# Key scales widened later, and another order of projections and mixer rows, in a hybrid decoder block

## The chip, the cores and the metric

The program runs on one core of one Trainium2 chip. The metric is the time of one execution in microseconds (us). A time is the median of several executions; beside it stand the lowest and the highest. A profile is one further execution, recorded by the hardware profiler, with a time of its own.

The engines of the core are named as the profile names them: PE (TensorE, matmuls and transposes; PEld its weight loads), DVE (VectorE), ACT (ScalarE), POOL (GpSimd) and SP (which issues nearly all DMAs).

## What is computed

One layer of a decoder on 512 tokens of width 2048, all float32. `h = rms_norm(x)` is multiplied by one matrix of 30 column tiles of 128; their outputs feed three token mixers:

```python
proj = h @ w_in[l]
aq, ak, av, bu, bg, cq, ck, cv = jnp.split(proj, splits, axis=-1)
aq = _rms_norm(aq.reshape(B, S, A_HEADS, HEAD_DIM), a_q_g[l])
ak = _rms_norm(ak.reshape(B, S, A_HEADS, HEAD_DIM), a_k_g[l])
out_a = _dilated_mixture(aq, ak, av)              # 8 heads of 64, three dilations
out_b = _conformer_conv(bu, bg, ...)              # GLU, 31 taps, layer norm, silu
cq, ck = (_rms_norm(...) for both)
out_c = _band_attention(cq, ck, cv, 127, sinks)   # 16 query heads, 2 key heads
mix = jnp.concatenate([out_a, out_b, out_c], axis=-1)
x = x + mix @ w_out[l]
h2 = _rms_norm(x, norm2_g[l])
x = x + (silu(h2 @ w_gate[l]) * (h2 @ w_up[l])) @ w_down[l]
```

Queries and keys are normalised per head: each is divided by the root of the mean of its own squares. This is the "scale" in what follows.

## The kernel before

Activations lie transposed: 128 channels on the partitions, 512 tokens along a row. A float32 product is made of three matmuls on a high and a low part of each operand (`mm3`, lines 312 to 314: high weights by high data, high by low, low by high). ACT makes a high part by rounding, and DVE (POOL for the C rows of the mixer) makes the low part by subtracting it.

**Projections.** `PROJ` is the order of the 30 column tiles: a letter for the mixer, a letter for the kind (q, k, v, u, g) and a number. The first four run ahead. Each of the others is a loop over 16 k tiles, three matmuls each (`project`). The host lays out the weights in the order of `PROJ`, so the loads stay a straight stream in whatever order it stands.

**Ticks.** Everything that is not a projection is hung between its matmuls by a clock written out by hand. After every second k tile (six matmuls) `project` calls `ticks.tick()`, and `ticks.after(n, fn)` makes `fn` issue its instructions n ticks from now. A projection has 8 ticks. Each engine runs its instructions in the order in which they were issued, and waits where an operand isn't there.

**A key tile** (`do_k`, with `head_scales`) is a chain of such steps: ACT copies the tile out of PSUM (L564, `raw`); SQ = 3 ticks later PE transposes it (L569, `f`); then one tick each: ACT squares (L574), DVE sums per head (L579, L581), POOL raises the sums to the power -1/2 (L586, `r`). Then `then(r)` hangs up the widening: ACT spreads each scale over the 64 channels of its head (L623, `wide`); a tick later PE transposes that (L630, `t`), a tick later DVE multiplies the raw keys by it (L636), a tick later SP copies each half to the other partitions (L642, the twin, two DMAs), and TD = 2 ticks later ACT and DVE make the high and the low part (L648, L653). `box["k at"]` tells the heads the tick from which they may use the key. A query tile (`do_q`) is split without its scale (L602, L607, four DMAs L609, L610), which goes into the exponent instead.

**Heads.** C heads come in pairs of query tiles that share a key (`grouped_attention`), A heads one tile at a time (`attention`): scores on PE (L755 to L758), maxima on DVE (L770 to L786), exps on ACT (L796), denominators on DVE (L803 to L808), normalising on POOL (L811, L814), transposes on PE (L846, L916), their high and low parts (L852, L857; L921, L927, L933), and the product with the values (L870, L871, L946). A head starts at the earliest tick at which its key, its query and its values are ready and the head before it is far enough ahead. Names: `a1o` is the output of A tile 1, `a1pl` the low part of its weights, `a10s` the scores of its head 0, `ml_c` the low part of a mixer row tile of C. PSUM has six rotating banks for all this, and a seventh and eighth for the projections; an allocation waits for the last reader of the bank that it gets.

**Output projection.** `ROWS` is the order in which the 16 row tiles of the mixed output enter the contraction with `w_out` (again the host lays the weights out in this order). The first eight form half 0, the others half 1. The first two output tiles run together (`first_two`), one tick after each k, which is six matmuls; after them four k tiles, 12 matmuls, go to a tick. `split_rows(k)` makes the high and low parts of rows k to k + 2 that exist by then. Rows ahead of that are split during the last projection.

Past the mixer come the feed-forward matmuls (lines 1255 and 1397), to which the change does nothing.

Of the kernel before, what the change touches and what calls it, by code (L numbers as in the profile page):

```python
# [36 lines left out]
PAUSE_FROM, TAP_PAUSE = 205, 9  # L37


SQ, VD, TD, EV = 3, 4, 2, 1  # L40


C_TICKS = (1, 6, 2, 2, 2, 2, 4, 1, 5)
# [1 line left out]


PROJ = ("av0 av1 av2 av3 bu0 bg0 cv ck cq0 cq3 bu1 bg1 cq1 cq5 cq2 "
        "cq7 bu2 bg2 ak2 cq4 cq6 bu3 bg3 ak0 aq0 ak1 aq1 aq2 ak3 aq3").split()
ROWS = "c0 c1 c2 c4 c5 c3 c7 c6 a0 a1 b2 b1 b0 b3 a2 a3".split()

N_SLOTS = 67
N_WIDE = 4
# [70 lines left out]
def kernel(ctx: ExitStack, tc: tile.TileContext, xT, wi, wo, wgu, wd, cst_in, outT):  # L123
# [19 lines left out]
    ticks = Ticks()  # L143

    def slot(name, dt=F32, cols=T):
        return sp.tile([P, cols], dt, name=name, tag="s")
# [4 lines left out]
    def bank(name, cols=T):  # L151
        return psum["banks"].tile([P, cols], F32, name=name, tag="b")
# [116 lines left out]
    at = {"entry": 0, "split": 0, "use": 0}  # L269
# [208 lines left out]
    def project(name):  # L478
        b = column(name)
        for half in range(2):  # L480
            wh, wl = next_unit()
            for kk in range(8):
                k = 8 * half + kk
                s = slice(kk * P, (kk + 1) * P)
                mm3(b, wh[:, s], wl[:, s], h_hi[k], h_lo[k], k == 0, k == KT - 1)
                if kk % 2 == 1:
                    ticks.tick()
        return b
# [61 lines left out]
    def ln_out(mix):  # L550
# [3 lines left out]
        for j in range(NB):  # L554
            nc.scalar.activation(yconv[j], yconv[j], AF.Silu, bias=col(C_LB + j), scale=col(C_LG + j))
            mix[f"b{j}"] = yconv[j]
        for n, name in enumerate(r for r in ROWS if r[0] == "b"):
            ticks.after(1 + n, split_mix, name)


    def head_scales(b, name, then):

        raw = slot(name + "raw")
        nc.scalar.copy(raw, b)  # L564

        def flip():
            b2 = bank(name + "f")
            for i in range(NT):
                nc.tensor.transpose(b2[:, i * P:(i + 1) * P], raw[:, i * P:(i + 1) * P], ident)  # L569
            ticks.after(1, square, b2)  # L570

        def square(b2):
            sq = slot(name + "sq")
            nc.scalar.activation(sq, b2, AF.Square)  # L574
            ticks.after(1, total, sq)

        def total(sq):
            v = cp.tile([P, NT, 2], F32, name=name + "v", tag="hsv", bufs=3)
            nc.vector.tensor_reduce(v.rearrange("p a b -> p (a b)"), sq.rearrange("p (a b) -> p a b", b=HD),  # L579
                                    axis=mybir.AxisListType.X, op=ALU.add)  # L580
            nc.vector.tensor_add(v, v, c64[:, :, None].to_broadcast([P, NT, 2]))  # L581
            ticks.after(1, power, v)

        def power(v):
            r = cp.tile([P, NT, 2], F32, name=name + "r", tag="hsr", bufs=4)
            nc.gpsimd.tensor_tensor(r, v, nhalf.rearrange("p (a b) -> p a b", b=2), op=ALU.pow)  # L586
            then(r)

        ticks.after(SQ, flip)
        return raw  # L590

    def do_q(box, b, name):
        def then(r):
            box["rq"] = r

        raw = head_scales(b, name, then)
        box["q at"] = ticks.now + SQ + 4
        q = box["q"] = [slot(f"{name}{h}", F32R) for h in range(2)]

        def high():  # L600
            hi = slot(f"{name}hi", F32R)
            nc.scalar.copy(hi, raw)  # L602
            ticks.after(1, low, hi)

        def low(hi):
            lo = slot(f"{name}lo", F32R)
            nc.vector.tensor_sub(lo, raw, hi.bitcast(F32))  # L607
            for h in range(2):
                nc.sync.dma_start(q[h][HALF[h]].bitcast(F32), hi[HALF[h]].bitcast(F32))  # L609
                nc.sync.dma_start(q[h][HALF[1 - h]].bitcast(F32), lo[HALF[h]].bitcast(F32))  # L610
        ticks.after(1, high)

    def do_k(box, b, name, gi):
        def then(r):
            ticks.after(2, widen, r)

        raw = head_scales(b, name, then)
        box["k at"] = ticks.now + SQ + TD + 10
        both = []

        def widen(r):
            wide = slot(name + "wide")
            nc.scalar.copy(wide.rearrange("p (a b c) -> p a b c", a=NT, b=2),  # L623
                           r[:, :, :, None].to_broadcast([P, NT, 2, HD]))
            ticks.after(1, flip, wide)

        def flip(wide):
            b2 = bank(name + "t")
            for i in range(NT):
                nc.tensor.transpose(b2[:, i * P:(i + 1) * P], wide[:, i * P:(i + 1) * P], ident)  # L630
            ticks.after(1, scale, b2)

        def scale(b2):
            for h in range(2):
                both.append(slot(f"{name}{h}"))
                nc.vector.scalar_tensor_tensor(both[h][HALF[h]], raw[HALF[h]], gqk[HALF[h], gi:gi + 1], b2[HALF[h]],  # L636
                                               op0=ALU.mult, op1=ALU.mult)
            ticks.after(1, twin)

        def twin():  # L640
            for h in range(2):
                nc.sync.dma_start(both[h][HALF[1 - h]], both[h][HALF[h]])  # L642
            ticks.after(TD, high)

        def high():
            box["k"] = [(slot(f"{name}h{h}", F32R), slot(f"{name}l{h}", F32R)) for h in range(2)]
            for h in range(2):
                nc.scalar.copy(box["k"][h][0], both[h])  # L648
            ticks.after(1, low)

        def low():
            for h, (hi, lo) in enumerate(box["k"]):
                nc.vector.tensor_sub(lo, both[h], hi.bitcast(F32))  # L653
            if gi == 1:
                box["k0"] = [slot(f"{name}0{h}", F32R, 2 * P) for h in range(2)]
                for k0, src in zip(box["k0"], both):
                    nc.scalar.copy(k0[:, :P], src[:, :P])
                    nc.vector.tensor_sub(k0[:, P:], src[:, :P], k0[:, :P].bitcast(F32))
# [327 lines left out]
    def split_mix(name):  # L986
        if name not in m_hi:
            m = mix.pop(name)
            hi, lo = slot(f"mh_{name}", F32R), slot(f"ml_{name}", F32R)
            nc.scalar.copy(hi, m)  # L990
            (nc.gpsimd if name[0] == "c" else nc.vector).tensor_sub(lo, m, hi.bitcast(F32))  # L991
            m_hi[name], m_lo[name] = hi, lo
# [26 lines left out]
    for name in PROJ[HEAD4:]:  # L1019
        kind, what, j = name[0], name[1], name[2:]  # L1020
        if name == PROJ[-1]:
            for n, row in enumerate(ROWS[:2]):
                ticks.after(4 + n, split_mix, row)
        b = project(name)
        if kind == "b":
            ticks.after(0, glu if what == "g" else glu_u, int(j), b)
            continue
        if kind == "c":
            box = Heads(shared) if j else shared
        else:  # L1030
            box = boxes.setdefault(j, {})
        if what == "k":
            do_k(box, b, name, 1 if kind == "c" else 0)
        elif what == "v":
            do_v(box, b, name)
        else:
            do_q(box, b, name)
        if what == "q":
            if kind == "a":
                load_v(box, int(j))  # L1040
                attention(boxes.pop(j), kind + j)
                continue
            waiting.append((box, kind + j, (int(j), int(j) + 8)))
            if len(waiting) == 2:
                grouped_attention(waiting)
                waiting = []
# [6 lines left out]
    def load_x(i):  # L1053
        if i < KT:
            n = OUT_ORDER[0][i]
            xr[n] = slot(f"xr{n}")
            nc.sync.dma_start(xr[n], xT[n])
# [79 lines left out]
    def split_rows(k):  # L1137
        for name in ROWS[k:k + 3]:
            if name in mix:
                split_mix(name)  # L1140

    def first_two(*ns):
        two = [((bank if i else column)(f"o0_{n}"), *next_unit(SPLIT_AHEAD - i)) for i, n in enumerate(ns)]
        for k in range(8):
            row = ROWS[k]
            while row not in m_hi and row not in mix:
# [13 lines left out]
    for half in range(2):  # L1160
        for i, n in enumerate(OUT_ORDER[half]):
# [12 lines left out]
            for kk in range(8):  # L1174
                if half == 1 and i == KT - 2 and kk == 4:
                    first_sum[0][0]()
                k = 8 * half + kk
                row = ROWS[k]
                while row not in m_hi and row not in mix:
# [7 lines left out]
            if half == 0:  # L1187
                load_x(i + 2)
                if i >= 8 and ROWS[i] in mix:
                    split_mix(ROWS[i])  # L1190
# [337 lines left out]
    for g in range(2 * NP + N_DOWN):  # L1528
# [8 lines left out]
        for i, q in enumerate(ORDER):  # L1537
# [35 lines left out]
            if N_TURNED - 2 <= t < N_TURNED:  # L1573
                n = 4 - (t % 2 == 0)
# [91 lines left out]
```

## Time and profile before

| | |
|---|---|
| median of 3 runs | 1879.83 us (1879.47 to 1881.76) |
| profiled execution | 1881.01 us, of which the recorded span is 1879.0 |
| granted clock, mean | 0.998 |
| projections and mixer | to about 400 us |
| output projection | about 399 to 610 us |

The span is the time from the first to the last recorded instruction; the execution has 2.0 us around it. The views used below are: the page's busy times and chain; the waits of PE (which instruction stood idle, and which engine's instruction released it); the timelines, in which a row has the start and the duration in us, the engine, the line, the operation, out<-in, and in brackets the idle time before it and its releaser; windows, which give for a stretch of time the busy us and the count of instructions of PE, PEld, DVE, ACT and POOL, the clock granted to PE as a share of full speed (PEclk), the busy share of the DMA engines and GB/s; and groups of equal instructions (busy us in all, mean ns of one, idle before).

### The profile page before, as it was taken

What the parts mean: (1) busy time and instruction counts of PE and PEld (TensorE: products, weight loads), DVE (VectorE), ACT (ScalarE), POOL (GpSimd) and SP (SyncE); (2) the same over time, 40 slices, a digit from 0 to 9 for tenths busy, and PEclk for the clock granted to TensorE, in tenths of its full rate; (3) what the DMA queues carried; (4) which work ended last, traced back from release to release, by engine and by line L of the source; (5) the groups of instructions that cost most, each with busy time, mean ns of one, the idle gap of its engine ahead of it and who ended that gap; (6) DMA issues with size and microseconds to landing.
All of it is one profiled execution on the core that took longest, in us unless ns stands there. A gap on an engine that the chain in (4) does not pass through costs nothing.

```text
span 1879.0 us, 28424 instructions
## 1 busy us (share of the span) xinstructions
PE 1868.2 (99%) x9784; PEld 1605.4 (85%) x9784; DVE 1458.2 (78%) x2347; ACT 1333.2 (71%) x1886; POOL 1219.5 (65%) x812
## 2 busy tenths in 40 slices
PE   9999999999999999999999999999999999999999
PEld 7888878888888888888888888888888888888888
DVE  7578988997679777777777777777777677778887
ACT  6345545553556888888878888788887887777675
POOL 5014433462155878787877878788787867766786
PEclk9999999999999999999999999999999999999999
DMA  7333332434342354443544435344455475578984
GB/s 271 122 110 108 93 96 85 126 100 145 107 146 88 120 175 145 157 168 130 182 138 163 163 133 183 134 164 161 142 178 192 152 239 184 197 251 285 308 243 124
DMA packets 157984, 301.07 MB, mean 160 GB/s; under 512 B 29968, under 2 KB 69008, under 8 KB 157840
## 3 DMA queue, kind: packets, MB, share of 16 engines
q1 hardware_dynamic: 157696, 299.25, 48.4%
q8 instruction: 77, 1.26, 0.3%
q14 instruction: 67, 0.55, 0.1%
q10 hardware_dynamic: 144, 0.01, 0.0%
HBM read 241.27 MB, written 50.33 MB: 155 GB/s over the span
## 4 chain that ended last, share of the span: by engine, by line
PE 92%; DVE 5%; ACT 1%; issue 1%; POOL 1%; DMA 0%; DVEq 0%; POOLq 0%; ACTq 0%
PE out L1255 51%; PE out L1397 16%; PE o L313 3%; PE o L314 3%; PE o L312 3%; DVE wl L290 1%; PE cq L312 1%; PE cq L314 1%; PE cq L313 1%; DVE y L514 1%; PE in L313 1%; PE in L312 1%; PE in L314 1%; PE ak L314 1%; PE ak L312 1%
## 5 line engine op out<-in xcount | busy, mean ns | idle before, releaser
L1255 PE MATMUL out<-h,wh 128*128 128x512 f32 x2464 | 588.4, 391 | 0.0
L1255 PEld LDWEIGHTS out<-h,wh 128*128 128x128 f32 x2464 | 452.7, 188 | 87.5
L1255 PEld LDWEIGHTS out<-h,wl 128*128 128x128 f32 x2464 | 316.1, 191 | 12.5 <-DVE wl L295 0.4
L1255 PE MATMUL out<-h,wl 128*128 128x256 f32 x2464 | 320.3, 283 | 0.2 <-DVE wl L295 0.2
L1397 PE MATMUL out<-wh,a 128*128 128x512 f32 x896 | 221.2, 389 | 0.0
L1397 PEld LDWEIGHTS out<-wh,a 128*128 128x128 f32 x896 | 168.2, 188 | 34.9
L289 ACT CAST wh<-w 128x1024 fp32r<-128x1024 f32 (+1 forms) x93 | 96.8, 1042 | 129.3 <-PE o L313 43.2
L290 DVE TENSOR_TENSOR wl<-w,wh 128x1024 fp32r<-128x1024 f32 (+1 forms) x93 | 117.1, 1261 | 44.9 <-ACT wh L289 44.5
L1397 PE MATMUL out<-wl,a 128*128 128x512 f32 x448 | 119.7, 389 | 0.0
L1397 PEld LDWEIGHTS out<-wl,a 128*128 128x128 f32 x448 | 84.1, 188 | 17.4
L514 DVE SCALAR_TENSOR_TENSOR y<-bu,cst,y 128x511 f32<-128x511 f32 (+14 forms) x120 | 94.4, 787 | 0.7
L1255 PE MATMUL out<-a,wh 128*128 128x512 f32 x330 | 80.1, 391 | 0.0
L1255 PEld LDWEIGHTS out<-a,wh 128*128 128x128 f32 x330 | 60.3, 188 | 11.4
L312 PE MATMUL o<-mh_c,wh 128*128 128x512 f32 x128 | 51.2, 400 | 0.0
L313 PE MATMUL o<-ml_c,wh 128*128 128x512 f32 x128 | 50.1, 392 | 0.5 <-POOL ml_c L991 0.5
L314 PE MATMUL o<-mh_c,wl 128*128 128x512 f32 x128 | 50.1, 391 | 0.0
L1442 DVE TENSOR_TENSOR Y<-Y,out 128x512 f32<-128x512 f32 x48 | 30.7, 682 | 19.4 <-PE out L1397 19.3
L1255 PEld LDWEIGHTS out<-a,wl 128*128 128x128 f32 x330 | 43.3, 191 | 2.2
L1255 PE MATMUL out<-a,wl 128*128 128x256 f32 x330 | 44.1, 283 | 0.0
L312 PE MATMUL cq<-hh,wh 128*128 128x512 f32 x96 | 39.3, 410 | 0.0
L430 POOL TENSOR_TENSOR ssum<-ssum,sq 128x512 f32<-128x512 f32 x15 | 26.8, 1785 | 19.1 <-ACT sq L429 18.6
L314 PE MATMUL cq<-hh,wl 128*128 128x512 f32 x96 | 38.3, 399 | 0.0
(3395 smaller groups left out, 5170.7 us busy)
## 6 DMA issues: line engine op xcount, KB each, us to landing
od<-a SPq DMA_DIRECT2D x140, 256.0 KB, 4.7
a<-od SPq DMA_DIRECT2D x140, 256.0 KB, 6.4
w<-in_wi SPq DMA_DIRECT2D x59, 512.0 KB, 3.6
w<-in_wo SPq DMA_DIRECT2D x32, 512.0 KB, 3.5
x<-in_xT SPq DMA_DIRECT2D x16, 256.0 KB, 7.4
xr<-in_xT SPq DMA_DIRECT2D x16, 256.0 KB, 3.7
x2d<-xr SPq DMA_DIRECT2D x16, 256.0 KB, 2.0
yd<-z SPq DMA_DIRECT2D x16, 256.0 KB, 5.3
```

Of the source, the lines that this page charges most:

```text
L289: nc.scalar.copy(hi[:, :n], t[:, :n])
L290: eng.tensor_sub(lo[:, :n], t[:, :n], hi[:, :n].bitcast(F32))
L312: nc.tensor.matmul(out, wh, xh, start=start, stop=False)
L313: nc.tensor.matmul(out, wh, xl, start=False, stop=False)
L314: nc.tensor.matmul(out, wl, xh, start=False, stop=stop)
L430: eng.tensor_add(acc, acc, sq)
L514: nc.vector.scalar_tensor_tensor(yconv[j][:, i:], hconv[j][:, :T - i], c, yconv[j][:, i:], op0=ALU.mult, op1=ALU.add)
L1255: nc.tensor.matmul(out, lhs[:, s], rhs, start=begin, stop=last and low == flip[0] and x is xs[-1], skip_group_check=True)
L1397: nc.tensor.matmul(to[h], x[:, h * P:(h + 1) * P], v[:, j], start=sub == 0 and h not in started, stop=sub == 1 and n in (len(todo) - 1, le ...
L1442: nc.vector.tensor_add(t, t, b)
```

## The change

The widening of every key's scales is hung up KW = 5 ticks after the power instead of 2, and `box["k at"]` counts these ticks, so it stands 20 ticks after the projection instead of 15. In `PROJ` ak0 goes ahead of bu3 and bg3, aq2 ahead of ak3, and aq1 behind ak3. In `ROWS` the C rows stand in the order of the pairs of query tiles (c0 c3, c1 c5, c2 c7, c4 c6), and of the A rows a2 goes ahead of a1. During the last projection three rows are split, at ticks 1, 3 and 5, instead of two, at ticks 4 and 5. No operation is added or removed.

```diff
-SQ, VD, TD, EV = 3, 4, 2, 1
+SQ, KW, VD, TD, EV = 3, 5, 4, 2, 1
...
 PROJ = ("av0 av1 av2 av3 bu0 bg0 cv ck cq0 cq3 bu1 bg1 cq1 cq5 cq2 "
-        "cq7 bu2 bg2 ak2 cq4 cq6 bu3 bg3 ak0 aq0 ak1 aq1 aq2 ak3 aq3").split()
-ROWS = "c0 c1 c2 c4 c5 c3 c7 c6 a0 a1 b2 b1 b0 b3 a2 a3".split()
+        "cq7 bu2 bg2 ak2 cq4 cq6 ak0 bu3 bg3 aq0 ak1 aq2 ak3 aq1 aq3").split()
+ROWS = "c0 c3 c1 c5 c2 c7 c4 c6 a0 a2 b2 b1 b0 b3 a1 a3".split()
...
     def do_k(box, b, name, gi):
         def then(r):
-            ticks.after(2, widen, r)
+            ticks.after(KW, widen, r)
 
         raw = head_scales(b, name, then)
-        box["k at"] = ticks.now + SQ + TD + 10
+        box["k at"] = ticks.now + SQ + KW + TD + 10
...
         if name == PROJ[-1]:
-            for n, row in enumerate(ROWS[:2]):
-                ticks.after(4 + n, split_mix, row)
+            for n, row in enumerate(ROWS[:3]):
+                ticks.after(1 + 2 * n, split_mix, row)
```

What it does to the order is shown at two places. The first is ACT's queue at ak2's widening (`ak2wide`), in the middle of the C heads; `c71` is the second head of C tile 7 and `cq4` a query tile. Before:

```order
L564 COPY cq4raw_2511<-cq4_2357 128x512
L289 CAST wh43_2516<-w43_1973 128x1024
L623 COPY ak2wide_2528<-ak2r_2494 128x512
L796 ACTIVATE c71e0_2503,c71d_1899<-c71s1_2467,c71d_1899,cq7r_2037 128x128 x2
L798 ACTIVATE c71d_1899<-c71d_1899,cst_75 128x2
L602 CAST cq4hi_2543<-cq4raw_2511 128x512
L289 CAST wh44_2599<-w44_2059 128x1024
```

After the change:

```order
L564 COPY cq4raw_2511<-cq4_2357 128x512
L289 CAST wh43_2516<-w43_1973 128x1024
L796 ACTIVATE c71e0_2503,c71d_1899<-c71s1_2467,c71d_1899,cq7r_2037 128x128 x2
L798 ACTIVATE c71d_1899<-c71d_1899,cst_75 128x2
L602 CAST cq4hi_2541<-cq4raw_2511 128x512
L623 COPY ak2wide_2581<-ak2r_2494 128x512
L289 CAST wh44_2588<-w44_2059 128x1024
```

ak2wide stands behind the exps of c71 and the rounding of cq4 instead of ahead of them. PE's queue at the transposes of it (`ak2t`), before:

```order
L313 MATMUL cq6_2515<-h3_188,wh41_2358 128x512
L314 MATMUL cq6_2515<-h3_188,wl41_2359 128x512
L630 MATMUL ak2t_2545<-ident_110,ak2wide_2528 128x128 x4
L312 MATMUL cq6_2515<-hh4_214,wh41_2358 128x512
L313 MATMUL cq6_2515<-hl4_215,wh41_2358 128x512
L314 MATMUL cq6_2515<-hh4_214,wl41_2359 128x512
```

and after the change:

```order
L946 MATMUL c20o1_2569<-c20bh1_2474,cvd0_855 128x256 x2
L946 MATMUL c20o1_2569<-c20bl1_2492,cvd0_855 128x256 x2
L569 MATMUL cq4f_2583<-ident_110,cq4raw_2511 128x128 x4
L312 MATMUL cq6_2515<-hh8_311,wh42_2426 128x512
L313 MATMUL cq6_2515<-hl8_312,wh42_2426 128x512
L314 MATMUL cq6_2515<-hh8_311,wl42_2427 128x512
L312 MATMUL cq6_2515<-hh9_338,wh42_2426 128x512
L313 MATMUL cq6_2515<-hl9_339,wh42_2426 128x512
L314 MATMUL cq6_2515<-hh9_338,wl42_2427 128x512
L630 MATMUL ak2t_2605<-ident_110,ak2wide_2581 128x128 x4
L312 MATMUL cq6_2515<-hh10_359,wh42_2426 128x512
L313 MATMUL cq6_2515<-hl10_360,wh42_2426 128x512
```

ak2t has moved behind the rest of that half of cq6's projection, behind the products of head 0 of the C pair c2, c7 (`c20o`), the transposes of cq4 and six more matmuls.

The second place is DVE's queue early in the output projection, where the second A head pair's weights get their low parts. Before, this pair is a1's and the scores beside it are a2's:

```order
L781 ISA a20s2_4092,a20d_3688<-a20s2_4092,bias_a_122 128x512
L781 ISA a20d_3688 128x1
L784 SCALAR_TENSOR_TENSOR a20d_3688<-a20d_3688,aq2r_3841 128x1
L607 TENSOR_TENSOR aq3lo_4130<-aq3raw_4019,aq3hi_4095 128x512
L636 SCALAR_TENSOR_TENSOR ak30_4136<-ak3raw_3855,gqk_124,ak3t_4097 64x512
L636 SCALAR_TENSOR_TENSOR ak31_4138<-ak3raw_3855,gqk_124,ak3t_4097 64x512
L675 TENSOR_TENSOR av30_4124<-av3s_4023,av30_4124 128x4x64
L675 TENSOR_TENSOR av31_4125<-av3s_4023,av31_4125 128x4x64
L884 TENSOR_TENSOR mix_a1_4128<-mix_a1_4128,a1o0_4080 64x512
L806 SCALAR_TENSOR_TENSOR a20e1_4155,a20d_3688<-a20e1_4155,mult_a_121 128x384
L808 RECIPROCAL a20d_3688<-a20d_3688 128x1
L857 TENSOR_TENSOR a1pl10_4194<-a1t10_4112,a1ph10_4162 128x512
```

After the change the pair is a2's and the scores are a1's:

```order
L607 TENSOR_TENSOR aq3lo_4144<-aq3raw_4033,aq3hi_4111 128x512
L884 TENSOR_TENSOR mix_a2_4113<-mix_a2_4113,a2o0_4076 64x512
L806 SCALAR_TENSOR_TENSOR a10e0_4132,a10d_3856<-a10e0_4132,mult_a_121 128x128
L806 SCALAR_TENSOR_TENSOR a10e0_4132,a10d_3856<-a10e0_4132,mult_a_121 128x256
L808 RECIPROCAL a10d_3856<-a10d_3856 128x2
L781 ISA a10s2_4135,a10d_3856<-a10s2_4135,bias_a_122 128x512
L781 ISA a10d_3856 128x1
L784 SCALAR_TENSOR_TENSOR a10d_3856<-a10d_3856,aq1r_4022 128x1
L675 TENSOR_TENSOR av30_4138<-av3s_4037,av30_4138 128x4x64
L675 TENSOR_TENSOR av31_4139<-av3s_4037,av31_4139 128x4x64
L857 TENSOR_TENSOR a2pl10_4180<-a2t10_4104,a2ph10_4142 128x512
L857 TENSOR_TENSOR a2pl11_4198<-a2t11_4127,a2ph11_4176 128x512
```

The scaling of ak3 (L636) is no longer here, and the first low part of the second head (`a2pl10`, before `a1pl10`) follows the two low parts of av3 at once. On PE the scores a10s2 and the transposes `aq3f`, which take the bank that a2pl10 reads, stand as follows after the change:

```order
L757 MATMUL a10s2_4135<-ak1h0_3704,aq10_3852 128x512
L758 MATMUL a10s2_4135<-ak1l0_3705,aq10_3852 128x512
L312 MATMUL o0_0_4062<-mh_c5_4094,wh61_3859 128x512
L313 MATMUL o0_0_4062<-ml_c5_4095,wh61_3859 128x512
L314 MATMUL o0_0_4062<-mh_c5_4094,wl61_3860 128x512
L312 MATMUL o0_1_4069<-mh_c5_4094,wh62_3951 128x512
L313 MATMUL o0_1_4069<-ml_c5_4095,wh62_3951 128x512
L314 MATMUL o0_1_4069<-mh_c5_4094,wl62_3952 128x512
L846 MATMUL a2t12_4161<-ident_110,a21e1_3934 128x128
L846 MATMUL a2t12_4161<-ident_110,a21e2_3987 128x128
L569 MATMUL aq3f_4171<-ident_110,aq3raw_4033 128x128 x4
L312 MATMUL o0_0_4062<-mh_c2_4117,wh61_3859 128x512
```

Before, `aq3f` took the bank of the scores a20s1, which ACT's exps read last.

## The prediction

> **What bounds the kernel now.** I read the page first (busy times, chain), then the waits of PE, then the timelines at each wait.
>
> ```profile
> PE 1868.2 (99%) x9784; PEld 1605.4 (85%) x9784; DVE 1458.2 (78%) x2347; ACT 1333.2 (71%) x1886; POOL 1219.5 (65%) x812
> ...
> PE 92%; DVE 5%; ACT 1%; issue 1%; POOL 1%; DMA 0%; DVEq 0%; POOLq 0%; ACTq 0%
> ```
>
> PE is busy for 1868.2 us of the span and carries 92% of the chain that ended last. The change leaves PE's matmuls as they are, so it can only win or lose time in which PE stands still, or runs at a lower clock. The view of PE's waits lists nearly all of the first kind (engine, line waited for: us in total, times, longest):
>
> ```profile
> core 0 of [0], span 1879.0 us
> ...
> PE ak2t L630 <- ACT ak2wide L623: 3.8, 1, 3.8
> PE idle L410 <- DVE bones L343: 1.4, 1, 1.4
> PE ak1t L630 <- ACT ak1wide L623: 0.8, 1, 0.8
> PE a10s L758 <- DVE ak1l L653: 0.8, 1, 0.8
> PE o L313 <- POOL ml_c L991: 0.5, 2, 0.3
> ```
>
> The 1.4 us are at the start, before anything that is changed. The other four lie in the mixer and at the start of the output projection, and each waits for a step that the change moves: 3.8 + 0.8 + 0.8 + 0.5 = 5.9 us. The first costs more than it shows. PE's timeline (start, duration):
>
> ```profile
> 253.75 0.39 PE L313 MATMUL cq<-h,wh 128*128 128x512 f32 x1
> 253.98 0.39 PE L314 MATMUL cq<-h,wl 128*128 128x512 f32 x1
> 258.21 1.12 PE L630 MATMUL ak2t<-ident,ak2wide 128*128 128x128 f32 x4 [3.84 <-ACT ak2wide L623]
> ...
> 263.88 0.40 PE L946 MATMUL c20o<-c20ph,cv 128*128 128x256 f32 x2
> ...
> 265.55 0.60 PE L569 MATMUL cq4f<-ident,cq4raw 128*128 128x128 f32 x4
> ...
> 391.14 0.60 PE L846 MATMUL a1t<-ident,a10e 128*128 128x128 f32 x4
> 391.57 0.60 PE L569 MATMUL ak3f<-ident,ak3raw 128*128 128x128 f32 x4
> ```
>
> A 128x512 matmul issues every 0.23 us (253.75 to 253.98; 0.2265 over longer stretches), four transposes take 0.43 us (391.14 to 391.57). Between the matmul at 253.98 and c20o stand four transposes and 12 matmuls: 0.43 + 12 x 0.2265 = 3.15 us. Without a stall c20o would start at 253.98 + 0.23 + 3.15 = 257.36; it started at 263.88, 6.5 us late. The rest beyond the 3.84 us is the clock (windows: us, busy times and counts, PEclk, DMA share, GB/s):
>
> ```profile
> 254.37:258.20 3.83, 0.00 (x0) 0.00 (x0) 3.69 (x9) 0.66 (x2) 3.13 (x2) 0.79 0.00 0
> 258.20:260.00 1.80, 1.79 (x7) 1.60 (x8) 0.27 (x2) 1.54 (x6) 0.61 (x1) 0.50 0.81 232
> ...
> 256.50:257.00 0.50, 0.00 (x0) 0.00 (x0) 0.50 (x1) 0.00 (x0) 0.50 (x1) 0.59 0.00 0
> ...
> 263.40:263.80 0.40, 0.40 (x3) 0.35 (x2) 0.00 (x0) 0.00 (x0) 0.30 (x1) 0.98 0.83 190
> ```
>
> The granted clock fell to half at about 256.6, 2.2 us after PE's last matmul ended (254.37), and came back at about 263.4. The 5.2 us of work from 258.21 on ran at half speed, which is 2.6 us lost. The wait at the start (1.4 us) and those of 0.8 us show no such drop.
>
> **The change, part by part.**
>
> *ak2's widening, three ticks later.* Why it was late:
>
> ```profile
> 254.21 1.69 POOL L933 TENSOR_TENSOR c20bl<-c20pl,mask_c 128x512 fp32r<-128x512 f32 x1 [1.36 <-DVE c20pl L927]
> 255.87 1.63 POOL L586 TENSOR_TENSOR ak2r<-ak2v,nhalf 128x8 f32<-128x8 f32 x1
> ...
> 257.54 0.62 ACT L623 COPY ak2wide<-ak2r 128x512 f32<-128x512 f32 x1 [3.49 <-POOL ak2r L586]
> 258.06 0.45 ACT L796 ACTIVATE c71e<-c71s,c71d,cq7r 128x128 f32<-128x128 f32 x1
> ...
> 259.13 0.61 ACT L602 CAST cq4hi<-cq4raw 128x512 fp32r<-128x512 f32 x1
> ```
>
> ACT stood 3.49 us on ak2r, and the exps of c71 and cq4hi were queued behind it. In the changed order both go ahead of ak2wide. They then end before ak2r does, or little after: c71e to cq4hi took 259.74 - 258.06 = 1.7 us here, from about 256.2 (when DVE ends c71's maximum) that gives 257.9. ak2wide then ends near 258.5. PE reaches ak2t only after 12 matmuls (2.72), c20o (265.55 - 263.88 = 1.67), four transposes (0.43) and 6 matmuls (1.36): 254.21 + 6.18 = 260.4. That is 1.9 us to spare; without it the wait returns by as much as ak2wide is later. Gain: 6.5 us.
>
> Where the stall goes: DVE worked for 3.69 of the 3.83 us in which PE stood, and now does that work beside PE. The next thing due is c20bl for c20o's second tile: POOL ended it at 255.90, PE wants it at about 254.2 + 2.72 + 1.4 = 258.3, 2.4 us to spare. I take nothing for it, with 2 us as the bad end.
>
> *ck three ticks later* moves the first C heads by 18 matmuls, 4.1 us. On SP's queue ck's two twin DMAs are now issued behind three weight loads instead of ahead of them, and the heads start ten ticks after, as before. The heads' mixer rows are read some 200 us later, so I take nothing; if DVE, on which their maxima wait, falls back by it, at most those 4.1 us less what the heads' spacing holds. *ak0 before bu3, bg3* brings its two scalings and two low parts (2.8 us of DVE) ahead of c40o:
>
> ```profile
> 312.77 2.87 POOL L933 TENSOR_TENSOR c40bl<-c40pl,mask_c 128x256 fp32r<-128x256 f32 x2 [1.02 <-DVE c40pl L927]
> ...
> 318.49 0.40 PE L946 MATMUL c40o<-c40bl,cvd 128*128 128x256 f32 x2
> ```
>
> POOL was done at 315.64, 2.85 us early, as much as the added work: 0 to 1 us, I take 0.2. ak0's two twin DMAs on SP go with it; aq0 is their next reader, far behind.
>
> *ak1 later, aq2 sooner, aq1 later.* ak1's transposes come 5 ticks after the power instead of 2, against a wait of 0.8; the second pair of A heads now uses ak2, whose low part is 100 us old, in place of ak1's, another 0.8. Both go: 1.6 us. aq2's DMAs are issued with aq2, as aq1's were; same distance.
>
> *Three rows split at ticks 1, 3, 5* takes one more ml_c out of POOL's full stretch behind tick 5 and puts the first two some 5 us further ahead of their matmuls: 0.5 us, or nothing if POOL falls behind again.
>
> *What the order costs.* ak3 (scaling, sums, low part) moves some 14 us up, into the stretch where DVE is fullest (two windows, then groups of DVE between 340 and 420):
>
> ```profile
> 340.00:370.00 30.00, 28.44 (x140) 23.36 (x139) 27.99 (x73) 16.29 (x30) 11.37 (x9) 1.00 0.41 115
> 370.00:395.00 25.00, 25.00 (x133) 21.20 (x132) 24.26 (x64) 12.86 (x22) 12.01 (x9) 1.00 0.30 85
> ...
> L806 DVE SCALAR_TENSOR_TENSOR a20e<-a20e,mult_a 128x128 f32<-128x128 f32 (+3 forms) x4 | 1.9, 482 | 0.0
> ...
> L636 DVE SCALAR_TENSOR_TENSOR ak<-ak3raw,gqk,ak3t 64x512 f32<-64x512 f32 x2 | 1.5, 742 | 0.0
> ...
> L653 DVE TENSOR_TENSOR ak3l<-ak,ak3h 128x512 fp32r<-128x512 f32 x2 | 1.3, 679 | 0.0
> ```
>
> DVE had 0.74 us free in the last 25 there, and takes 1.5 + 1.3 us more, with about 0.8 for ak3's sums: 3.6 us. Two dues are near. The output of the second A head pair waits for its last low part:
>
> ```profile
> 400.33 0.41 DVE L857 TENSOR_TENSOR a1pl<-a1t,a1ph 128x256 fp32r<-128x256 f32 x1
> ...
> 402.87 0.28 PE L871 MATMUL a1o<-a1pl,av 128*128 128x256 f32 x1
> ```
>
> That was 2.1 us early: 0 to 1.5, I take 0.1. And aq3f's transposes take a PSUM bank that DVE's a2pl frees, which stands on DVE behind the maxima of a10's third part and two av low parts; PE does those scores just eight instructions earlier. The like steps here:
>
> ```profile
> 403.22 0.39 PE L758 MATMUL a20s<-ak2l,aq 128*128 128x512 f32 x1
> ...
> 403.65 0.70 DVE L781 CUSTOM_DVE_ANT_0 a20s<-a20s,bias_a 128x512 f32<-128x512 f32 x1 [0.24 <-PE a20s L758]
> ...
> 407.82 0.76 DVE L675 TENSOR_TENSOR av<-av3s,av 128x256 fp32r<-128x256 f32 x2
> ...
> 409.89 0.69 DVE L857 TENSOR_TENSOR a1pl<-a1t,a1ph 128x512 fp32r<-128x512 f32 x1
> ```
>
> From the score's start DVE needs 0.43 + 0.70 + about 0.25 for its two small followers + 0.76 + 0.69 = 2.8 us; PE has 7 matmuls and two transposes, 1.8 us. So aq3f waits 1.0 us even if DVE is on time, and 1.0 + 3.6 - 0.7 = 3.9 if all of ak3's work makes it late. I take 1.3, near the low end, since DVE stood idle 0.24 us at this very place. Queued behind it on PE is the output projection.
>
> **Sum:** 6.5 + 1.6 + 0.5 = 8.6 won, 1.3 + 0.2 + 0.1 = 1.6 lost: 7.0 us. The profiled execution took 1881.01 us (its span and 2.0 around it), which gives 1874.0. It lies 1.2 above the median of 1879.83; some of that may be a longer low clock in this execution, so I keep 1874.0 and do not take 7.0 off the median (1872.8).
>
> **Rivals.**
>
> *The clock never fell in the timed executions.* Then 2.6 us of the gain are the profile's alone: 1879.83 - (7.0 - 2.6) = 1875.4. The one row that there is speaks against: 2.2 us of idling did it, and the 3.84 us stall was longer. By the Trainium skill ("TensorE: Matmul & The Clock Gate", the part on the HAM clock gate) it takes an idle window of about 3.4 us on a free-running grid, so a 3.84 us stall would hold a whole one only about once in eight placements, an estimate. The trace agrees on the grid (256.6 to 263.4 is 6.8 us, two such windows) and not on the whole idle window. Chance 0.08.
>
> *The stall only moves within the C stage.* DVE keeps the 3.7 us that it used to catch up, and c20o's second tile or ak2t waits 2 to 3 us: 1881.01 - 7.0 + 2.5 = 1876.5. For it: ACT and POOL both hang on DVE there; against it: the 1.9 and 2.4 us counted above. Chance 0.13.
>
> *DVE is late through the A stage.* aq3f waits 3.9 us in place of 1.3, and this is longer than 2.2, so the clock falls for 2.6 more: 7.0 - 2.6 - 2.6 = 1.8 won, 1879.2; below 2.2 us of waiting the clock stays. Without the clock it is 1876.6. Chance 0.13 for both, a third with the clock.
>
> *Slower.* The same bank wait, with ak3's and a21's norms (four of 0.48 us) ahead of it as well: 1.0 + 3.6 + 1.9 = 6.5 us, and a longer low clock of up to 3.4: 9.9 + 0.3 against 8.6, 1882.6. It decides from a wait of 5.7 us on. Against it: nothing in this trace let DVE fall so far behind near 400. Chance 0.05.
>
> *It doesn't do what it says:* cq4hi or the exps on ACT hold ak2wide as late as ak2r did, and the gain elsewhere is eaten: 1879.8. Chance 0.05.
>
> **How the numbers follow.** The forecast has 0.56: 1874.0, itself between 1872 (no new wait, 8.6 off the profiled execution, or 7.8 off the median) and 1876 (3 us more waits). A measurement of this kernel tells 0.2%, 3.76 us, from no change: faster means under 1876.07. From the forecast 0.55 is faster, from the clock rival 0.06, from the moved stall 0.06, from the late DVE 0.05: 0.72. Slower by so much needs 1883.6, which is the slower rival's upper half and what I have not thought of: 0.05. Same 0.23. The range leaves out the slower case, the unchanged one and part of the rest: 1871.6 to 1878.8.
>
> **What would show it.** Right: no wait at ak2t, the clock at 1.00 through 250 to 270, c20o near 257.4; no wait at ak1t nor for an A head's low part; a wait of about 1 us at aq3f, released by DVE L857. Wrong: a wait over 2 us anywhere between 250 and 420 with PEclk at 0.50 after it; waits at c40o or at the first A outputs; DVE without idle time from 300 to 400. After 610 us the two traces should be the same, shifted.

## The result and the profile after

The changed kernel takes 1885.88 us (median of 8 runs, 1885.05 to 1886.56) against 1880.14 for the kernel before beside it (8 runs): a ratio of 1.0029, interval 1.0018 to 1.0040. It is 5.7 us slower where 6 were forecast to be won. Its profiled execution has a span of 1884.1 us, 5.1 above the one before.

PE's waits after the change (engine, line, waited for: us, times, longest):

```profile
core 0 of [0], span 1884.1 us
...
PE a2t L846 <- DVE mix_a L884: 2.8, 1, 2.8
PE aq3f L569 <- DVE a2pl L857: 2.7, 1, 2.7
PE ak0t L630 <- ACT ak0wide L623: 1.9, 1, 1.9
PE idle L410 <- DVE bones L343: 1.4, 1, 1.4
PE a2o L871 <- DVE a2pl L857: 1.3, 1, 1.3
PE a10s L757 <- ACT a10e L796: 0.7, 1, 0.7
PE ak3f L569 <- DVE mix_a L884: 0.6, 1, 0.6
```

All four waits of before are gone. Six new ones stand for them: 2.8 + 2.7 + 1.9 + 1.3 + 0.7 + 0.6 = 10.0 us, against 5.9. The clock in windows of the same profile:

```profile
250.00:270.00 20.00, 20.00 (x106) 16.91 (x105) 19.46 (x41) 11.22 (x26) 11.30 (x10) 1.00 0.41 119
...
304.00:306.00 2.00, 2.00 (x7) 1.59 (x6) 2.00 (x2) 1.00 (x3) 1.29 (x1) 0.50 0.04 8
306.00:308.00 2.00, 2.00 (x9) 1.77 (x9) 1.86 (x9) 0.00 (x0) 1.42 (x2) 0.70 0.86 258
...
408.00:410.00 2.00, 0.41 (x2) 0.20 (x2) 1.97 (x8) 0.37 (x1) 0.35 (x1) 0.90 0.31 66
410.00:412.00 2.00, 0.00 (x0) 0.00 (x0) 1.97 (x7) 0.00 (x0) 2.00 (x3) 0.50 0.93 177
...
414.00:418.00 4.00, 4.00 (x16) 3.22 (x15) 2.24 (x3) 1.49 (x3) 3.63 (x3) 0.70 0.01 2
```

Through ak2t (250 to 270) PE is busy without a gap and the clock is full. But it falls to half twice elsewhere. From about 303.8 to 307.2 it costs half of 3.4 us, 1.7. From about 409.6 to 416.4 PE stands until 412.07 and works for 4.3 us at half speed, 2.2. With the waits that is 13.9 us, against 5.9 + 2.6 = 8.5 before: 5.4 more, where the spans differ by 5.1. Where time lost to the low clock is given below, it is PE's busy time times the share of the clock that was missing, summed over windows of 0.2 us from 200 to 620 us.

The stall at ak0t, from the timelines of POOL, ACT and PE:

```profile
294.35 2.06 POOL L586 TENSOR_TENSOR ak0r<-ak0v,nhalf 128x8 f32<-128x8 f32 x1
...
301.24 0.46 ACT L796 ACTIVATE c41e<-c41s,c41d,cq4r 128x128 f32<-128x128 f32 x1 [2.51 <-DVE c41d L786]
...
302.31 0.61 ACT L623 COPY ak0wide<-ak0r 128x512 f32<-128x512 f32 x1
...
302.97 0.66 PE L630 MATMUL ak0t<-ident,ak0wide 128*128 128x128 f32 x4 [1.86 <-ACT ak0wide L623]
```

ak0's scale was ready at 296.4, but on ACT its widening now stands behind the exps of c41, and those wait 2.51 us for DVE's maximum. It is the stall at ak2t again, with the places of the two exchanged.

The stalls around 400 us, from DVE, POOL and PE:

```profile
400.07 1.67 POOL L586 TENSOR_TENSOR aq1r<-aq1v,nhalf 128x8 f32<-128x8 f32 x1
401.70 3.60 POOL L991 TENSOR_TENSOR ml_c<-mix_c,mh_c 128x512 fp32r<-128x512 f32 x2
...
401.77 1.25 DVE L784 SCALAR_TENSOR_TENSOR a10d<-a10d,aq1r 128x2 f32<-128x2 f32 x1 [2.08 <-POOL aq1r L586]
...
405.25 2.35 DVE L653 TENSOR_TENSOR ak3l<-ak,ak3h 128x512 fp32r<-128x512 f32 x2
...
408.13 0.67 DVE L884 TENSOR_TENSOR mix_a<-mix_a,a2o 64x512 f32<-64x512 f32 x1
...
408.94 0.41 PE L846 MATMUL a2t<-ident,a21e 128*128 128x128 f32 x2 [2.82 <-DVE mix_a L884]
...
411.24 1.27 DVE L857 TENSOR_TENSOR a2pl<-a2t,a2ph 128x512 fp32r<-128x512 f32 x2
...
412.07 1.09 PE L569 MATMUL aq3f<-ident,aq3raw 128*128 128x128 f32 x4 [2.72 <-DVE a2pl L857]
```

DVE itself stands for 2.08 us, with work queued, because aq1's scale (`aq1r`) isn't there. Behind that wait, in DVE's order, come mix_a and a2pl, each of which frees the PSUM bank that PE's next transposes need. Between the wait and mix_a stand also ak3's two low parts (`ak3l`, 2.35 us), which the new order has brought there.

Why aq1r is late shows in ACT's copies of the query tile whose heads run third. Before this is aq2, in the changed kernel aq1 (the first row is of before, the second of after):

```profile
367.24 0.59 ACT L564 COPY aq2raw<-aq 128x512 f32<-128x512 f32 x1 [0.71 <-PE aq L314]
```

```profile
379.69 0.59 ACT L564 COPY aq1raw<-aq 128x512 f32<-128x512 f32 x1 [3.73 <-PE aq L314]
```

The third pair's first scores ran at 395.4 before (a20s) and at 393.1 after (a10s). The query had been copied 28 us before that and is now copied 13 us before: it comes a whole projection later, its heads do not.

### The profile page after: what moved, and what is told of

It reads as the page before. It is cut to its first block, busy times and chain, and to the rows that moved or that the text cites. A ratio compares the mean times of both kernels' runs of the same rounds, so it can differ in the third digit from the quotient of the medians.

```text
span 1884.1 us, 28424 instructions
## 1 busy us (share of the span) xinstructions
PE 1869.3 (99%) x9784; PEld 1607.1 (85%) x9784; DVE 1461.4 (78%) x2347; ACT 1332.6 (71%) x1886; POOL 1220.5 (65%) x812
## 4 chain that ended last, share of the span: by engine, by line
PE 90%; DVE 7%; issue 1%; ACT 1%; POOL 0%; DMA 0%; DVEq 0%; ACTq 0%; POOLq 0%
PE out L1255 51%; PE out L1397 16%; PE o L312 3%; PE o L313 3%; PE o L314 3%; DVE y L514 1%; DVE wl L290 1%; PE in L313 1%; PE in L314 1%; PE cq L314 1%; PE cq L312 1%; PE cq L313 1%; PE in L312 1%; PE aq L312 1%; PE aq L313 1%
```

## The experiments

The theories: **A1**, aq1 comes too late for its heads; **A2**, ak0's move makes the stall at ak0t and delays DVE; **B**, DVE has no time to spare, so a stall taken away at one place comes back at another; **K**, the later keys move the A heads too far down; **P**, POOL's two-input operations hold DVE up. "KW = 5" stands for the change's lines in `do_k`.

### KW = 5 alone

```diff
-SQ, VD, TD, EV = 3, 4, 2, 1
+SQ, KW, VD, TD, EV = 3, 5, 4, 2, 1
...  ticks.after(KW, widen, r);  box["k at"] = ticks.now + SQ + KW + TD + 10
```

> The kernel before with one part of the change alone: the widening 5 ticks after the power (KW = 5), projections and rows in the old order. Theory A (the part works as forecast, the loss of the change comes from the order of the projections): the wait at ak2t with its low clock (6.5 us) and the one at ak1t (0.8) go, the A heads start up to 7 us later because their key is ready later, which costs at most 1 to 2 us at the start of the output projection: 1873 to 1876 us. Theory B (DVE is the bound: the stall at ak2t was DVE's chance to catch up, and without it the same time is lost later whatever the order): new waits of 4 us and more between 260 and 420 us, 1879 to 1882.

1880.97 us (10 runs), ratio to the kernel before 1.0002 (0.9993 to 1.0011). PE's waits:

```profile
PE a0o L871 <- DVE a0pl L857: 1.7, 1, 1.7
...
PE o L312 <- ACT mh_a L990: 1.3, 1, 1.3
PE a3o L871 <- DVE a3pl L857: 1.2, 1, 1.2
PE o L313 <- POOL ml_c L991: 1.2, 1, 1.2
PE c40o L946 <- POOL c40bl L933: 0.6, 1, 0.6
```

The waits at ak2t, ak1t and a10s went, and nothing was won: by its time B. But the new waits (6.0 us in all) are small ones, spread over the mixer and half 1 of the output; 3.5 of them stand between 260 and 420 us, where B had put 4 and more. The clock fell to half behind a0o and again behind mh_a, 3.4 us lost in all; this execution, 1882.72 us, is the longest of the ten.

### The A part of the order put back

```diff
-... ak0 bu3 bg3 aq0 ak1 aq2 ak3 aq1 aq3        ROWS: ... a0 a2 b2 b1 b0 b3 a1 a3
+... ak0 bu3 bg3 aq0 ak1 aq1 aq2 ak3 aq3        ROWS: ... a0 a1 b2 b1 b0 b3 a2 a3
```

> The changed kernel with the A part of the order put back: ak1 aq1 aq2 ak3 aq3, and rows a0 a1 ... a2 a3. The widening, ak0's place, the C rows and the three early splits stay. Theory A1 (aq1 comes a projection too late for its heads, DVE stands 2.1 us for its scale, and the waits from 397 to 412 us follow from that): the 8.1 us of waits there and the low clock after them (about 2.2 us) go, the wait at ak0t stays: 1875 to 1877. Theory A2 (ak0's move is the cause, it makes DVE late from 300 on): waits of 3 us and more remain between 340 and 420, 1881 or more. Theory B (DVE the bound): the same, 1880 to 1884.

1881.85 us, 4.0 below the changed kernel. The waits around 400 went down to one of 1.5 us for ml_c, as A1 has it, and ak0t kept its 1.9. But a3o and mh_a (1.2 and 1.3 us) came as with KW = 5 alone, so the time is 5 us above A1's and in A2's and B's ranges. Their sign, a wait of 3 us or more between 340 and 420, did not come.

### ak0 put back

```diff
-... ak0 bu3 bg3 aq0 ak1 aq2 ak3 aq1 aq3
+... bu3 bg3 ak0 aq0 ak1 aq2 ak3 aq1 aq3
```

> The changed kernel with ak0 put back behind bu3 and bg3; aq2, ak3, aq1 stay in the new order. The wait of 1.9 us at ak0t and the low clock after it (about 1.7 us) should go in any theory, unless ak0t waits at its old place too. Theory A1 (aq1 too late): the waits of the A stage stay, as a10's scores still stand close behind aq1: 1881 to 1884. Theory A2 (ak0's move makes DVE late): they go too, 1874 to 1877. Theory B: 1880 to 1883.

1880.09 us, 5.8 below the changed kernel, at the lower end of B's range and below A1's. The wait at ak0t went, and of those around 400 one of 2.7 us stayed, at a10's first scores (396.25). The profile names no releaser for it. aq1 stands in the same late place here, but its layout DMAs were issued up to 385.2 and took 2.2 to 4.6 us to land, well ahead of it. DVE's mix_a, which frees a bank as at a2t, ends at 396.15, 0.1 us ahead of the scores; that it released them is likely but not shown. A low clock beside this wait cost 3.1 us.

### The whole old order, with KW = 5, paired C rows and early splits

> The changed kernel with the whole old order of projections and of the A rows: KW = 5, the C rows in pairs and three early splits remain. Theory A (both moves in the order cost, the rest gains): no wait over 1 us between 230 and 420, the waits for ml_c gone: 1873 to 1875, and 0.3 to 0.6 us under the kernel with KW = 5 alone. Theory B (DVE the bound): 1879 to 1882.

1879.94 us, 0.9997 (0.9987 to 1.0006): B's range. The same waits as with KW = 5 alone, but ml_c at 0.3 instead of 1.2. The medians lie 1.0 us apart, with ranges that overlap.

### aq1 ahead of ak3

```diff
-... ak0 bu3 bg3 aq0 ak1 aq2 ak3 aq1 aq3
+... ak0 bu3 bg3 aq0 ak1 aq2 aq1 ak3 aq3
```

> The changed kernel with aq1 ahead of ak3 again (ak1 aq2 aq1 ak3 aq3); all else as changed. Theory A1 (the third pair's query comes a projection too late, so DVE stands for its scale): DVE's 2.1 us wait for aq1r goes, and with it the waits at a10s, a2t and most of aq3f, 5 us and 2 us of low clock: 1877 to 1880, with the 1.9 us at ak0t still there. Theory B (DVE has too much to do whatever the order): the waits only change their places, 1883 to 1886.

1879.09 us (1878.52 to 1879.32), 6.8 below the changed kernel: A1's range, and B is out for this part. PE's waits now:

```profile
PE ak0t L630 <- ACT ak0wide L623: 1.9, 1, 1.9
PE aq1f L569 <- DVE mix_a L884: 1.7, 1, 1.7
...
PE aq3f L569 <- DVE a2pl L857: 1.0, 1, 1.0
PE a2o L871 <- DVE a2pl L857: 0.9, 1, 0.9
```

aq3f waits the 1.0 us that the prediction had worked out for a DVE on time. DVE no longer waits for aq1r. The query is copied at 362.9 and a10s runs at 390.6, 27.7 us later. The exchange does a second thing: ak3's low parts no longer stand on DVE between a10's maxima and mix_a. This run doesn't part the two. Nor are the 6.8 us waits alone: between the two profiles PE stands 4.0 us less and loses 3.9 us less to the low clock, 1.7 of which lie at ak0t, where both kernels wait the same 1.9 us.

### aq1's heads two ticks later

```diff
-        box["q at"] = ticks.now + SQ + 4
+        box["q at"] = ticks.now + SQ + (6 if name == "aq1" else 4)
```

> The changed kernel, but aq1's query counts as ready two ticks later, so the heads of a1 (a10s and what follows) start 3.9 us of PE work later and DVE asks for aq1's scale later. Theory A1: DVE's wait for aq1r (2.1 us) and what follows from it (a2t 2.8, aq3f 2.7) shrink by 4 us or more: 1879 to 1882. Theory B: DVE fills the time with work that it is behind with, the waits at a2t and aq3f shrink by under 2 us: 1883 to 1886.

1885.14 us: 0.7 below, in B's range. DVE's wait for aq1r fell to 0.8 us, but a2t still waits 2.5, a2o 1.8 and aq3f 1.8. DVE now stands 3.3 us for a10's scores, which come behind a2o on PE, which itself waits for DVE. ak3's low parts (2.39 us) still stand ahead of mix_a. So the wait for aq1r is not what costs by itself; of the two ways to give aq1 more time, only bringing it sooner, which also takes ak3 out of the way, helped.

### Less load on DVE

```diff
         at_tap = TAPS_FROM + int(n * TAP_TICKS)
+        if at_tap >= 100 and 0 < i < TAPS - 1:
+            continue
```

The three kernels of this part leave out most taps of the convolution from tick 100 on, so their results are not the layer's; each was executed once. DVE is busy for 169.1 us between 200 and 420 us instead of 203.4 in the changed kernel: a sixth less, not a third. Few taps stand behind 395 us (13.1 us busy up to 410, against 12.7), so what leaving them out takes away there is DVE's backlog, not its load.

In the changed kernel:

> The changed kernel with most taps of the convolution left out from tick 100 (about 210 us) on, so the B rows are not the reference's: about 0.73 us of DVE less in every 2.2 us of PE work, a third of DVE's load. Theory B (every new wait is DVE's lateness): the waits at ak0t, a2o, a2t, ak3f and a10s go, aq3f keeps about the 1.0 us that its place behind a10s costs: span 1884.1 - 9 - 3.9 of low clock = about 1871. Theory A1 and A2 (the order makes chains too short): DVE's waits for POOL's powers stay, waits of 4 us and more remain, 1876 or more.

Span 1875.9 us, at the lower end of A1's and A2's view. PE's waits:

```profile
PE a2t L846 <- DVE mix_a L884: 2.5, 1, 2.5
PE aq3f L569 <- DVE a2pl L857: 2.5, 1, 2.5
```

ak0t, a2o, a10s and ak3f no longer wait: those were DVE's lateness (B, and the cause behind A2). a2t and aq3f stay nearly whole, with DVE's 2.1 us for aq1r and ak3l's 2.37 ahead of them: a backlog of DVE's doesn't make them, which leaves the order (A1) and ak3's work in that place.

In the kernel before:

> The kernel before with the same taps left out. Theory B: ak2t's wait of 3.84 us falls under 1 us, because DVE was some 4 us behind with c20pl and ak2v, and the 0.8 us waits go too: about 1871 to 1873. If POOL's queue alone made ak2r late, ak2t still waits 2.5 us or more: 1876 to 1879.

Span 1871.8 us, one execution of 1873.57. ak2t waits 0.8 us instead of 3.84, and the clock stays up. The stall that the change went after was DVE's lateness, 3 of 3.8 us. Two new waits for DVE came at a1t, 1.1 us (mix_a) and 0.5 (ak).

With KW = 5 alone:

> KW = 5 alone (as e1), with most taps of the convolution left out from tick 100 on, so the B rows are not the reference's. In e1 new waits came at a0o (1.7), a3o (1.2), mh_a (1.3), ml_c (1.2) and c40o (0.6). Theory B (all of them are DVE's lateness): they go, span about 1871. Theory K (the later key moves the A heads 7 us up to 13 us down, and the rows a3 and a1 come too late for the output projection): a3o and mh_a stay, 2 us or more, span 1873 to 1875.

Span 1874.8 us. The waits at a0o and c40o went (2.3 us, DVE's lateness), those at mh_a, a3o and ml_c stayed:

```profile
PE o L312 <- ACT mh_a L990: 1.3, 1, 1.3
PE a3o L871 <- DVE a3pl L857: 1.2, 1, 1.2
PE o L313 <- POOL ml_c L991: 1.2, 1, 1.2
```

3.7 us stay, in K's range. That DVE plays no part in them doesn't follow from this run: between 425 and 610 us, where a3o and mh_a stand, DVE is busy for 141.2 us with and without those taps. What shows K is the run with ak2 alone (below), which leaves the other keys as they were and has none of the three waits. `box["k at"]` counts KW, so every A head waits for it; a0's first scores came at 340.5 with KW = 5 for all keys and at 332.6 with it for ak2 alone. Later widening and later heads were not tried apart.

### KW = 5 for ak2 alone

```diff
-            ticks.after(2, widen, r)
+            ticks.after(5 if name == "ak2" else 2, widen, r)
...
-        box["k at"] = ticks.now + SQ + TD + 10
+        box["k at"] = ticks.now + SQ + TD + (13 if name == "ak2" else 10)
```

> The kernel before with ak2 alone widened 5 ticks after its power, every other key, the projections and the rows as before: the forecast's main term by itself. Forecast's view (the stall costs 6.5 us and 1.9 us are to spare): 1880.0 - 6.5 = 1873.5, the waits at ak1t, a10s and ml_c unchanged. Theory B (DVE did 3.69 us of overdue work during the stall, and what it feeds is late elsewhere instead): no wait at ak2t, and new waits of 2 to 4 us between 260 and 420: 1876 to 1879.

**1875.75 us** (11 runs), ratio 0.9976 (0.9967 to 0.9985): faster than both kernels, by 4.2 and 10.1 us, a small step but clear of the noise. PE's waits:

```profile
PE a1t L846 <- DVE ak L636: 1.2, 1, 1.2
PE a1t L846 <- DVE mix_a L884: 1.1, 1, 1.1
PE ak1t L630 <- ACT ak1wide L623: 0.8, 1, 0.8
PE a10s L758 <- DVE ak1l L653: 0.8, 1, 0.8
```

Both views are half right. The stall and its low clock are gone for good, and 2.3 us of new waits, all for DVE, stand 140 us further on, less the 0.5 for ml_c that went by itself: 6.5 - 2.3 + 0.5 = 4.7 expected from the rows, 4.2 measured. So new waits take back about a third of the gain, not all. By the rows they are not simply work that DVE put off:

```profile
401.94 2.87 DVE L675 TENSOR_TENSOR av<-av3s,av 128x256 fp32r<-128x256 f32 x2
...
405.58 0.44 PE L846 MATMUL a1t<-ident,a11e 128*128 128x128 f32 x2 [1.07 <-DVE mix_a L884]
```

The two low parts of av3, just ahead of mix_a, took 0.76 us before. Here they stand beside POOL's ml_c (401.82 to 404.53) and take 2.87, and so they do in the kernel before with the taps left out, which has the same two waits (0.5 and 1.1 us). That they would go with ml_c elsewhere was not tried.

With paired C rows and early splits on top:

> As e17, with the C rows in pairs and three rows split at ticks 1, 3 and 5. Forecast's view: 0.5 us less than e17 (the waits for ml_c). Theory B, and POOL's ml_c holding DVE up in its fullest stretch: within 0.5 us of e17 or slower.

1875.39 us (1875.08 to 1877.91), 0.9977: not to be told from ak2 alone. Rows and splits win nothing that can be measured here.

### ak0 widened later still

```diff
-            ticks.after(KW, widen, r)
+            ticks.after(KW + 3 * (name == "ak0"), widen, r)      (and "k at" with it; aq1 ahead of ak3)
```

> The kernel with aq1 ahead of ak3 again (e6), and ak0's widening 8 ticks after its power instead of 5. Theory A2 (ak0wide stands on ACT behind exps that wait for a late DVE, and three ticks are 4 us, more than the 1.9 of the wait): the wait at ak0t goes and nothing takes its place, as a0's heads begin long after: 1.9 us off, and in some executions the low clock after it: 1876.5 to 1877.5. Theory B (DVE is behind, the wait only moves): new waits between 300 and 345, time within 0.5 us of 1879.1.

1881.14 us, 2.0 above the kernel with aq1 ahead of ak3. The wait at ak0t went, as A2 says, and one of 3.9 us came at a00s, on the DMA that lays out aq0; there it had been 0.4. The time is above both ranges; the place, 333 us, is one that B named. DVE ends aq0's low part at the same time in both kernels (329.6 and 329.8), PE comes to a00s 2.2 us sooner, and the copies take 3.6 us instead of 2.3 to land. So the wait moved to the next thing that DVE makes, and grew by the slower copies, whose reason was not followed; a low clock behind it lost 1.7 us more.

### The C rows' low parts on DVE

```diff
-            (nc.gpsimd if name[0] == "c" else nc.vector).tensor_sub(lo, m, hi.bitcast(F32))
+            nc.vector.tensor_sub(lo, m, hi.bitcast(F32))
```

In the changed kernel:

> The changed kernel with the C rows' low parts (ml_c, L991) on DVE instead of POOL. In the changed kernel DVE's a10d (two columns, 0.16 us elsewhere) took 1.25 us and ak3l 2.35 for two (1.29 elsewhere) beside POOL's ml_c. Theory P (a two-input operation on POOL keeps DVE from starting, so each ml_c costs DVE about 1.1 us, more than the 0.68 that DVE needs to do it itself): a10d back to 0.16, ak3l to 1.3, the waits at a2t and aq3f shrink by 1.5 to 3 us together: 1882 to 1884. Theory Q (DVE was just late, the long rows are an accident): DVE gets 8 x 0.68 = 5.4 us more work in its fullest stretch and the waits grow: 1887 to 1891.

1885.52 us, no difference. In the rows P is right. The two instructions that had taken 1.25 and 2.35 us:

```profile
402.54 0.16 DVE L784 SCALAR_TENSOR_TENSOR a10d<-a10d,aq1r 128x2 f32<-128x2 f32 x1 [2.16 <-POOL aq1r L586]
...
405.10 1.29 DVE L653 TENSOR_TENSOR ak3l<-ak,ak3h 128x512 fp32r<-128x512 f32 x2
```

The waits only shift: a2t waits 0.9 instead of 2.8, aq3f 3.3 instead of 2.7, a2o 1.8 instead of 1.3. In all PE stands 1.5 us less and loses 1.9 us more to the low clock. As for the time, neither P nor Q came out.

With aq1 ahead of ak3 and the later ak0:

> e14 with the C rows' low parts on DVE as well. Theory P: the waits at aq3f and a2o and those of the output's start shrink a little, 0.5 to 1.5 us under e14: 1875 to 1877. Theory Q: 1 to 4 us over e14.

1883.48 us, 2.3 above the same kernel with the low parts on POOL: Q's range, but not by more waiting for DVE. PE stands 7.1 us in the one profile and 7.3 in the other; what grew is the time lost to the low clock, 4.8 us against 1.7. In the kernel before:

> The kernel before with the C rows' low parts on DVE. Theory P: the two waits for ml_c (0.5 us) go, DVE's rows beside them (a20d 1.30, aq3v 1.10, a tap 1.76) go back to 0.16, 0.17 and 0.74: 1878.5 to 1880. Theory Q: waits for DVE of 2 us and more appear from 395 on: 1882 to 1885.

1880.22 us, no difference, near P's range; the waits for ml_c went, and one of 1.3 us for DVE's ak3 came.

## Why the prediction was wrong

*What bounds the kernel, and the low clock*: right. PE sets the end: its idle time and what it lost to the low clock between 200 and 620 us, taken off the span, leave 1868.6 to 1871.9 us in all 17 profiles, whose spans go from 1871.8 to 1884.1. All four waits went, and at ak2t the low clock with them; the 8.6 us won were there.

*ak2t has 1.9 us to spare*: it was only just enough. Three rows of the changed kernel:

```profile
258.05 0.46 ACT L796 ACTIVATE c71e<-c71s,c71d,cq7r 128x128 f32<-128x128 f32 x1 [2.18 <-DVE c71d L786]
...
259.63 0.61 ACT L623 COPY ak2wide<-ak2r 128x512 f32<-128x512 f32 x1
...
260.38 0.60 PE L630 MATMUL ak2t<-ident,ak2wide 128*128 128x128 f32 x4
```

ak2wide ended at 260.2, 0.1 us ahead of ak2t; the step had put its end at 258.5. It took c71's exps as ready at 256.2, as before. They came at 258.05, because DVE was later. The stall had been DVE's time to catch up, as the step itself said, and it then took nothing for it; with ak2 alone 2.3 us of new waits came.

*ck later, ak0 sooner*: failed. Only c40o was priced (0.2), and c40o did not wait. ak0's own transposes were not looked at: its widening stands five ticks behind its power as ak2's does, and on ACT it falls behind c41's exps. 1.9 us and 1.7 of low clock. That this hangs on DVE is shown by the run with the taps left out, in which the wait is gone.

*ak1 later, aq2 sooner, aq1 later*: **the step that failed most.** It counted two waits that went and said of the queries only that aq2's DMAs keep their distance. That aq1 comes a projection later while its heads' place stays was never set against its scale, which POOL makes behind a21's normalising. The run that exchanges aq1 and ak3 and nothing else wins 6.8 us. That all of it is aq1's was not shown, because the exchange takes ak3's low parts out of that stretch too; the step on what the order costs had counted that work, but set it at 1.3 us at aq3f alone.

*aq3f, 1.0 us at least*: right as a floor (1.0 in that run), mis-sized as a value: 2.7 instead of 1.3. *a2o*: 1.3 instead of 0.1. *a2t* (2.8), *a10s* (0.7), *ak3f* (0.6): not in the sum.

*The later widening of the other keys* was priced as pure gain, 1.6 us. By the runs with KW = 5 for all keys (1880.97) and for ak2 alone (1875.75) it costs 5.2: the A heads start 7.9 us later, and waits come at a0o, a3o, mh_a and ml_c.

*The sum*: 1.6 us were set for all that the change costs; waits and low clock make 13.9.

*The rivals*: the slower one named the right place, aq3f, and DVE, but as work in DVE's queue alone, where a wait of DVE's own (2.1 us for aq1r) stands beside that work; 1882.6, with a chance of 0.05. "DVE is late through the A stage" was right for a2o, ak3f and a10s. The clock rival fell: each timed execution has its own mean clock on record, and beside the run with ak2 alone all 20 of the kernel before show 0.998 or 0.999, all 11 of ak2 alone 1.000. "DVE is late" also took the clock to stay up below 2.2 us of waiting, and that was wrong: at ak0t it fell after 1.9.

*What stays open*: how the two moves add up. Bringing aq1 ahead of ak3 wins 6.8 us, putting back ak0 5.8, and the whole old order 5.9, so the two cost together about what each costs alone; no run shows by which step ak0's place bears on a10's heads.

## What to carry to other kernels

When an engine that PE waits for is busy through the wait, taking the wait away can move part of it: here a third came back 140 us later. Delay the one late step only, not all steps of its kind, since each later step moves what hangs on it. When a schedule written by hand moves a producer, look up the distance to each of its consumers in the new order, small ones like a per-head scale too, and not just the waits that the old order had. A wait of an engine that is not the bound costs when what it holds up behind it frees buffers for the one that is.

## What the runs showed of the hardware

The clock falls after shorter waits than 2.2 us, and not always. The same wait of 1.9 us at ak0t left the clock at 0.96 over 300 to 340 in the changed kernel and at 1.00 in the run with aq1 ahead of ak3:

```profile
300.00:340.00 40.00, 38.14 (x188) 32.12 (x188) 34.99 (x68) 22.52 (x48) 20.24 (x14) 0.96 0.36 105
```

```profile
300.00:340.00 40.00, 37.77 (x194) 31.55 (x193) 34.99 (x68) 22.45 (x48) 20.27 (x14) 1.00 0.35 105
```

A wait of 1.7 us at a0o did it in one of two profiles (0.93 over 370 to 395 with KW = 5 alone, 1.00 with the old order, paired rows and splits). Two waits close together, 1.35 us for mh_a and 0.2 for ml_a, did it in two of four: the clock was at half from 513.8 to 517.2 with KW = 5 alone and from 512.2 to 515.6 with the A part put back. The single wait of 1.33 us at a2o in the changed kernel did not. The low stretches last 3.4 or 6.8 us. The Trainium skill ("TensorE: Matmul & The Clock Gate", on the HAM clock gate) has a free-running window of about 3.4 us, and these lengths agree with it; it asks for a whole idle window, and these waits were about half of one.

How much this does to a time shows in the mean clock of each execution. With KW = 5 alone the two executions at 1.000 took 1879.4 and 1879.6 us, the eight at 0.999 or 0.998 1880.6 to 1882.7. With the old order, paired rows and splits the four at 1.000 took 1878.5 to 1879.7, the six at 0.999 1879.9 to 1880.7. But the clock is not all that parts executions: the times of the kernel with the A part put back lie in two groups, 1879.7 to 1880.0 and 1881.4 to 1882.0, and all three of the lower group have 0.999, four of the seven of the upper 1.000. What parts these two groups is open.

POOL's ml_c, an operation with two inputs, holds up DVE. The 128x2 operation on DVE took 1.25 us while POOL's ml_c ran and 0.16 with ml_c elsewhere, ak3l's two 2.35 and 1.29. The move of ml_c to DVE is all that differs between the two kernels.
